# Silu as one ScalarE function, and a head's decay matrix made once and read back, in a gated-delta and retention block

## The chip, the core and the metric

The kernel runs on one core of one Trainium2 chip. Its engines are TensorE (PE in the profile, with PEld for its weight loads), VectorE (DVE), ScalarE (ACT), GpSimd (POOL) and SyncE (SP); each takes its instructions strictly in the order in which they are queued. The metric is the time of one execution in device microseconds (us), as the median of the runs. The kernel before takes 1379.87 us (median of 3 runs, 1377.66 to 1380.05).

## The reference, cut to what matters

One transformer layer on 512 tokens of 1024 features. One projection `xn @ w_in` gives the inputs of two branches. Branch A convolves its q, k and v along the tokens, puts them through silu, and runs a gated delta rule over 8 heads; branch B is a retention over 4 heads. Both are normed and multiplied by a silu gate:

```python
qkv = jax.nn.silu(causal_depthwise_conv(jnp.concatenate([qa, ka, va], axis=-1), conv_a))
...
decay = jnp.exp(jnp.where(causal, g_cum[..., :, None] - g_cum[..., None, :], -jnp.inf))
lower = jnp.where(strict, jnp.einsum('bhncd,bhnmd->bhncm', k_beta, k) * decay, 0.0)
...
attn = jnp.where(causal, jnp.einsum('bhncd,bhnmd->bhncm', q, k) * decay, 0.0)
...
oa = rmsnorm(oa, norm_a) * jax.nn.silu(za.reshape(b, s, A_HEADS, A_DV))
...
ob = rmsnorm(ob, norm_b.reshape(B_HEADS, B_DV)) * jax.nn.silu(gb.reshape(b, s, B_HEADS, B_DV))
```

The decay matrix of a head depends on the gate g alone and is used twice: with the keys (`lower`) and with the queries (`attn`). Two sigmoid gates, the output projection and an MLP with squared ReLU follow.

## The kernel before

All weight products are taken in three matmuls of a high and a low part (`mm3`, L83 to L85). A block of weights, 128 x 1024, is loaded on SP's queue into `raw` (L93, 2 buffers), cast by ACT into `whi` (L113) and subtracted by DVE into `wlo` (L114); whi and wlo have 3 buffers each. So every 24 matmuls PE needs one ACT cast and one DVE subtraction. Products land in 4 PSUM banks `mm`; 3 more banks `dl` and one bank `tr` serve the small products and the transpositions.

A scheduler orders the instructions of every engine by priority (program order, with the weight splits lifted by 200) and by its own model of durations, so each engine's queue interleaves several of the steps below. Where a tile has only one buffer, the writer of the next tile waits for all readers of the last.

Branch A is written in this order: `keys(0)` (heads 0 to 3), `base_inverse(0)`, `values_queries(0)`, `keys(1)` (heads 4 to 7), then for each pair of heads g2 = 0 to 3 `recurrence`, `values_queries(g2 + 1)`, `gated` and `ya_partial`. The steps that the change touches:

- `conv_silu` (L496), called 32 times on 128 x 512 (8 times in keys for kf, 16 for the values, 8 for qf). ACT copies the product into `c_raw` (L501) and scales it into `c_y` (L506), DVE adds three taps (L508), ACT takes the tanh of it into c_raw (L509), DVE makes (tanh + 1) * c_y (L512). The factor one half of silu(x) = x/2 * (tanh(x/2) + 1) sits in the conv weights (L417). PE then transposes the result into the one `tr` bank; for the keys ACT squares it (L523) and copies it into `kd` (L568), which frees that bank.
- `decays(h)` (L525): ACT scales a triangular mask by a column eight times (L531, tiles `tg`, 2 buffers, 4 for `ghi` and 4 for `glo`), PE sums it in two matmuls (L532), ACT takes the exp into `dt` (L534, one buffer). It is called twice for every head, in `keys` and again in `values_queries`: 16 calls.
- The readers of dt: in keys, four DVE products into `mt` (L587, named acc) and four into kd (L590) for each head; in values_queries four products into `at` (L706).
- `gate_rows` (L466), the gate of branch A, 16 tiles: tanh on ACT (L470), (tanh + 1) * z on DVE (L471), then the norm on DVE (L473). `gate` in `outputs` (L914), the gate of branch B, 16 tiles: tanh on ACT (L917), product on DVE (L918). Two tanh more, for the sigmoid gates (L958, L986), stay as they are.
- `double_blocks` uses the buffer of dt for its tile `y` as well.

The exp needs another function table of ACT than Sqrt or Ln; the program loads a table by an instruction of its own (ACT_TABLE_LOAD) wherever the next function is not in the one loaded.

Of the kernel before, what the change touches and what calls it, by code (L numbers as in the profile page):

```python
# [10 lines left out]
F32 = mybir.dt.float32  # L11
# [3 lines left out]
AF = mybir.ActivationFunctionType  # L15
ALU = mybir.AluOpType
# [3 lines left out]
P = 128  # L20
T = 512
# [39 lines left out]
def hybrid_block_kernel(ctx: ExitStack, tc: tile.TileContext, a: dict, out: bass.AP):  # L61
    nc = tc.nc
# [15 lines left out]
    dr = ctx.enter_context(tc.tile_pool(name="dr", bufs=2, space=DRAM))  # L78
# [237 lines left out]
    convw = cp.tile([P, P], F32, name="convw")  # L316
# [39 lines left out]
    with tc.tile_pool(name="xp", bufs=2) as xp:  # L356
# [59 lines left out]
        transpose(pv[:, 1, :], conv_in)  # L416
        nc.vector.tensor_scalar(convw, pv[:, 1, :], 0.5, None, ALU.mult)  # L417
        nc.scalar.copy(later, cmat[:, 2 * P : 3 * P])
# [47 lines left out]
    def gate_rows(pss, o_t, zt):  # L466

        for t in range(4):
            th = zt(t)
            nc.scalar.activation(th, pss[t], AF.Tanh, scale=0.5)  # L470
            nc.vector.scalar_tensor_tensor(th, th, 1.0, pss[t], ALU.add, ALU.mult)  # L471
            for ap, rs, cs in o_t(t):
                nc.vector.scalar_tensor_tensor(ap, ap, rs, th[:, cs], ALU.mult, ALU.mult)  # L473
# [22 lines left out]
    def conv_silu(ps, ch, dst, pool):  # L496
        raw = pool.tile([P, T + 3], F32, tag="c_raw", name="c_raw", bufs=2)
        nc.gpsimd.memset(raw[:, 0:3], 0.0)
        y = pool.tile([P, T], F32, tag="c_y", name="c_y", bufs=2)
        th = raw[:, 0:T]  # L500
        nc.scalar.copy(raw[:, 3 : T + 3], ps)  # L501

        def tap(j):
            return convw[:, j * 32 + ch : j * 32 + ch + 1]

        nc.scalar.activation(y, ps, AF.Copy, scale=tap(3))  # L506
        for j in (2, 1, 0):
            nc.vector.scalar_tensor_tensor(y, raw[:, j : j + T], tap(j), y, ALU.mult, ALU.add)  # L508
        nc.scalar.activation(th, y, AF.Tanh)  # L509
        if dst is None:  # L510
            dst = y
        nc.vector.scalar_tensor_tensor(dst, th, 1.0, y, ALU.add, ALU.mult)  # L512
        return dst
# [11 lines left out]
    def decays(h, pool):  # L525
# [7 lines left out]
        dt = pool.tile([P, 4, P], F32, tag="dt", name="dt")  # L533
        nc.scalar.activation(dt, pd.rearrange("p (c n) -> p c n", c=4), AF.Exp)  # L534
        return dt

# [10 lines left out]
    with tc.tile_pool(name="pa", bufs=1) as pa:  # L547
# [130 lines left out]
        def values_queries(g2, pool):  # L678
# [13 lines left out]
            at = pool.tile([P, 8, P], F32, tag="at", name="at")  # L692
            ssq = pool.tile([P, 8], F32, tag="ssq", name="ssq", bufs=2)
            pss = feature_major(w_in, xs, OFF_QA + h0 * P, 256, 8)
            for hh in range(2):
# [3 lines left out]
                sum_squares(to_tokens(qf[:, hh, :]), ssq[:, 4 * hh : 4 * hh + 4], junk)  # L699
                dt = decays(h, pool)  # L700
                pk = psx.tile([P, 4, P], F32, tag="dl", name="dl", bufs=3)
# [18 lines left out]
        def recurrence(g2, vq, pool):  # L720
# [67 lines left out]
            rstd = pool.tile([P, 8], F32, tag="rstd", name="rstd", bufs=2)  # L788
            nc.vector.scalar_tensor_tensor(rstd, rsqrt(v, 8, "o"), 0.5, rq, ALU.mult, ALU.mult)
            return Rows(  # L790
# [38 lines left out]
    with tc.tile_pool(name="pb", bufs=1) as pb_:  # L829
# [6 lines left out]
        def tmp(name):  # L836
            return pb_.tile([P, T], F32, tag="tm", name=name, bufs=8)
# [68 lines left out]
        def outputs(h, scs):  # L906
# [7 lines left out]
            def gate(t):  # L914
                g = gs[:, t, :]
                th = tmp("g_t")
                nc.scalar.activation(th, g, AF.Tanh, scale=0.5)  # L917
                nc.vector.scalar_tensor_tensor(g, th, 1.0, g, ALU.add, ALU.mult)  # L918

# [18 lines left out]
            rstd = pb_.tile([P, 4], F32, tag="rstd", name="rstd")  # L938
            nc.vector.tensor_scalar(rstd, rsqrt(v, 4, "b"), 0.5, None, ALU.mult)
            for t in range(4):  # L940
# [341 lines left out]
```

## Time and profile before

| | us |
|---|---|
| median of 3 runs | 1379.87 |
| lowest and highest run | 1377.66, 1380.05 |
| the profiled execution, its own time | 1375.68 |
| span from its first to its last instruction | 1374.0 |
| PE busy | 1351.5 |
| DVE busy | 914.0 |
| ACT busy | 652.4 |

The profile is one execution. Busy time is the time in which an engine had an instruction in work; matmuls are pipelined, so their durations overlap, and what one costs in a stream is the distance from its start to the next start. "The chain that ended last" follows the execution back from its last instruction, at each step to what released it. A line in the table of waits reads: this engine's instruction sat idle for that one.

### The profile page before, as it was taken

Reading aid. Unit: us, or ns where it says so; the run is one execution under the profiler, and the core shown is the slowest. Engines: PE = TensorE matmul, PEld = TensorE weight load, DVE = VectorE, ACT = ScalarE, POOL = GpSimd, SP = SyncE. Lnnn points to the kernel's source line nnn. Section 1 sums busy time; section 2 is a strip of 40 time slices with the busy share of each in tenths; the row PEclk is TensorE's granted clock in tenths of the full one; section 3 lists DMA queues with packets and bytes.
Section 4 is the critical chain, followed back from the end, with each engine's and each line's share of the span. In section 5 each row is a group of like instructions: output and inputs, shape, how many; then the busy total and the mean of one; then the engine's idle time right before and its main releaser. Section 6 shows DMA issues by size and latency. Waiting matters only on the chain.

```text
span 1374.0 us, 17717 instructions
## 1 busy us (share of the span) xinstructions
PE 1351.5 (98%) x6598; PEld 1108.3 (81%) x6598; DVE 914.0 (67%) x1599; ACT 652.4 (47%) x1202; POOL 110.6 (8%) x160
## 2 busy tenths in 40 slices
PE   8999999999999999999999999999999999999997
PEld 5888788778887888887888888888889788787886
DVE  5599889963665557567477577575775745828535
ACT  6777564624543323453453343343455646336441
POOL 1112300221012002000000100011101100000000
PEclk9999999999999999999999999999999999999999
DMA  5243625369458447785583872588739843525421
GB/s 161 77 139 120 193 81 172 120 140 241 109 122 173 109 145 163 182 249 180 132 269 112 199 252 93 157 218 176 209 124 233 215 150 104 193 92 166 130 88 62
DMA packets 101656, 214.70 MB, mean 156 GB/s; under 512 B 7135, under 2 KB 20593, under 8 KB 101058
## 3 DMA queue, kind: packets, MB, share of 16 engines
q1 hardware_dynamic: 85616, 170.41, 38.8%
q0 software_dynamic: 15232, 41.90, 16.9%
q8 instruction: 52, 0.85, 0.3%
q10 hardware_dynamic: 722, 1.25, 0.2%
q14 instruction: 34, 0.28, 0.1%
HBM read 207.77 MB, written 64.49 MB: 198 GB/s over the span
## 4 chain that ended last, share of the span: by engine, by line
PE 84%; DVE 9%; ACT 3%; DMA 3%; issue 1%; SPq 0%; DVEq 0%; ACTq 0%
PE mm L85 19%; PE mm L84 19%; PE mm L83 19%; PE mm L238 9%; PE dl L238 8%; PE tr L320 2%; DVE wlo L114 2%; DMA raw<-in_w_in_dram 1%; DVE c_y L508 1%; PE dl L85 1%; PE dl L84 1%; PE dl L83 1%; DVE ffq L1116 1%; ACT whi L113 1%; PE dl L772 1%
## 5 line engine op out<-in xcount | busy, mean ns | idle before, releaser
L114 DVE TENSOR_TENSOR wlo<-raw,whi 128x1024 fp32r<-128x1024 f32 x250 | 305.0, 1222 | 275.6 <-ACT whi L113 274.7
L113 ACT CAST whi<-raw 128x1024 fp32r<-128x1024 f32 x250 | 262.9, 1052 | 439.9 <-PE mm L84 252.5
L84 PE MATMUL mm<-actT,whi 128*128 128x512 f32 (+1 forms) x528 | 207.4, 393 | 1.2 <-DVE actT L354 1.2
L85 PE MATMUL mm<-actT,wlo 128*128 128x512 f32 (+1 forms) x528 | 208.4, 395 | 0.0
L83 PE MATMUL mm<-actT,whi 128*128 128x512 f32 (+1 forms) x528 | 207.0, 393 | 1.0 <-ACT actT L353 1.0
L83 PEld LDWEIGHTS mm<-actT,whi 128*128 128x128 f32 x528 | 100.0, 190 | 20.9 <-ACT actT L353 1.3
L84 PEld LDWEIGHTS mm<-actT,whi 128*128 128x128 f32 x528 | 100.0, 189 | 20.4 <-DVE actT L354 1.4
L85 PEld LDWEIGHTS mm<-actT,wlo 128*128 128x128 f32 x528 | 100.2, 190 | 18.9
L85 PE MATMUL mm<-hn,wlo 128*128 128x512 f32 (+1 forms) x288 | 105.4, 366 | 0.0
L84 PE MATMUL mm<-hn,whi 128*128 128x512 f32 (+1 forms) x288 | 105.3, 366 | 0.0
L83 PE MATMUL mm<-hn,whi 128*128 128x512 f32 (+1 forms) x288 | 105.3, 366 | 0.0
L83 PE MATMUL mm<-og,whi 128*128 128x512 f32 x256 | 99.7, 390 | 0.5 <-DVE zz L471 0.5
L84 PE MATMUL mm<-og,whi 128*128 128x512 f32 x256 | 99.6, 389 | 0.0
L85 PE MATMUL mm<-og,wlo 128*128 128x512 f32 x256 | 99.6, 389 | 0.0
L238 PE MATMUL mm<-whi,xsum 128*128 128x512 f32 x256 | 80.8, 389 | 0.0
L508 DVE SCALAR_TENSOR_TENSOR c_y<-c_raw,convw,c_y 128x512 f32<-128x512 f32 x96 | 70.6, 751 | 3.4 <-ACT c_y L506 2.8
L85 PEld LDWEIGHTS mm<-hn,wlo 128*128 128x128 f32 x288 | 54.3, 189 | 8.8
L83 PEld LDWEIGHTS mm<-hn,whi 128*128 128x128 f32 x288 | 54.3, 189 | 8.7
L83 PE MATMUL mm<-whi,actT 128*128 128x512 f32 x152 | 61.3, 403 | 0.0
L84 PEld LDWEIGHTS mm<-hn,whi 128*128 128x128 f32 x288 | 54.3, 189 | 8.6
L238 PE MATMUL dl<-whi,ffq 128*128 128x512 f32 x192 | 61.1, 389 | 0.0
L238 PE MATMUL dl<-whi,actT 128*128 128x512 f32 x192 | 61.1, 389 | 0.0
(331 smaller groups left out, 2543.8 us busy)
## 6 DMA issues: line engine op xcount, KB each, us to landing
raw<-in_w_in_dram SPq DMA_DIRECT2D x105, 512.0 KB, 4.0
raw<-sums SPq DMA_DIRECT2D x56, 512.0 KB, 4.3
raw<-in_w_up_dram SPq DMA_DIRECT2D x36, 512.0 KB, 4.2
sums<-in_w_in_dram SPq DMA_DIRECT2D x32, 512.0 KB, 5.1
sums<-sums POOLq DMA_DIRECT2D x28, 512.0 KB, 7.5
raw<-in_w_down_dram SPq DMA_DIRECT2D x26, 512.0 KB, 4.4
sums<-in_w_down_dram SPq DMA_DIRECT2D x24, 512.0 KB, 7.4
raw<-in_w_br_a_dram SPq DMA_DIRECT2D x16, 512.0 KB, 4.1
```

The costliest lines, as they stand in the source:

```text
L83: nc.tensor.matmul(ps, lh, rh, start=first, stop=False)
L84: nc.tensor.matmul(ps, lh, rl, start=False, stop=False)
L85: nc.tensor.matmul(ps, ll, rh, start=False, stop=last)
L113: nc.scalar.copy(hi[:, :n], raw[:, :n])
L114: nc.vector.tensor_tensor(lo[:, :n], raw[:, :n], hi[:, :n], ALU.subtract)
L238: m = nc.tensor.matmul(pss[t], lhs[i // 2], rhs[i % 2], start=first and k + i == 0, stop=k + i == 5, skip_group_check=not first,)
L320: nc.tensor.transpose(ps, src, ident)
L508: nc.vector.scalar_tensor_tensor(y, raw[:, j : j + T], tap(j), y, ALU.mult, ALU.add)
L772: nc.tensor.matmul(po[:, hh, :], at[:, 4 * hh + c, :], vn[:, hh, :], start=True, stop=True)
L1116: return nc.scalar.copy(dst[0], r), nc.vector.tensor_tensor(dst[1], r, dst[0], ALU.subtract)
```

## The change

Silu becomes one ACT function: in `conv_silu` it writes the result itself, in `gate_rows` it reads PSUM and writes zz, in `gate` it works in place. The DVE product behind it is gone in all three, and so are the halves (L417, L789, L939). `decays` also stores dt to device memory, on ACT's queue, and `values_queries` reads it back, on ACT's queue, into the buffers of `tg`, instead of making it again.

```diff
         transpose(pv[:, 1, :], conv_in)
-        nc.vector.tensor_scalar(convw, pv[:, 1, :], 0.5, None, ALU.mult)
+        nc.vector.tensor_copy(convw, pv[:, 1, :])
...
         for t in range(4):
             th = zt(t)
-            nc.scalar.activation(th, pss[t], AF.Tanh, scale=0.5)
-            nc.vector.scalar_tensor_tensor(th, th, 1.0, pss[t], ALU.add, ALU.mult)
+            nc.scalar.activation(th, pss[t], AF.Silu)
...
         y = pool.tile([P, T], F32, tag="c_y", name="c_y", bufs=2)
-        th = raw[:, 0:T]
...
-        nc.scalar.activation(th, y, AF.Tanh)
         if dst is None:
             dst = y
-        nc.vector.scalar_tensor_tensor(dst, th, 1.0, y, ALU.add, ALU.mult)
+        nc.scalar.activation(dst, y, AF.Silu)
         return dst
...
         dt = pool.tile([P, 4, P], F32, tag="dt", name="dt")
         nc.scalar.activation(dt, pd.rearrange("p (c n) -> p c n", c=4), AF.Exp)
+        kept_decays[h] = dr.tile([P, 4, P], F32, tag=f"dt{h}", name="dts", bufs=1)
+        nc.scalar.dma_start(kept_decays[h], dt)
+        return dt
+
+    kept_decays = {}
+
+    def decays_again(h, pool):
+        dt = pool.tile([P, 4, P], F32, tag="tg", name="dt", bufs=2)
+        nc.scalar.dma_start(dt, kept_decays[h])
         return dt
...
             ssq = pool.tile([P, 8], F32, tag="ssq", name="ssq", bufs=2)
+            dts = [decays_again(h0 + hh, pool) for hh in range(2)]
             pss = feature_major(w_in, xs, OFF_QA + h0 * P, 256, 8)
...
-                dt = decays(h, pool)
+                dt = dts[hh]
...
-            nc.vector.scalar_tensor_tensor(rstd, rsqrt(v, 8, "o"), 0.5, rq, ALU.mult, ALU.mult)
+            nc.vector.tensor_tensor(rstd, rsqrt(v, 8, "o"), rq, ALU.mult)
...
             def gate(t):
                 g = gs[:, t, :]
-                th = tmp("g_t")
-                nc.scalar.activation(th, g, AF.Tanh, scale=0.5)
-                nc.vector.scalar_tensor_tensor(g, th, 1.0, g, ALU.add, ALU.mult)
+                nc.scalar.activation(g, g, AF.Silu)
...
-            nc.vector.tensor_scalar(rstd, rsqrt(v, 4, "b"), 0.5, None, ALU.mult)
+            nc.vector.tensor_copy(rstd, rsqrt(v, 4, "b"))
```

The scheduler then orders the queues anew. In the changed kernel's numbering the Silu of conv_silu is L509, the exp L531, the store L533, the reading back L540, the masks L528, the two copies of the product L499 and L504.

On ACT at the start of keys(0), from the cast of a weight block to the second key's Silu, there stands before:

```order
L113 CAST whi<-raw 128x1024
L509 ACTIVATE c_raw<-c_y 128x512 x2
L534 ACTIVATE dt<-dl 128x512
L501 COPY c_raw<-mm 128x512
L523 ACTIVATE junk,ssk<-tr 128x128
```

and now, from the squares of the first key on (kf is the keys' result, junk the squares for its norm, kd the copy that frees the bank tr; the first load and the Silus of the first two keys stand directly behind the same cast, six rows ahead of this piece):

```order
L499 COPY c_raw<-mm 128x512
L520 ACTIVATE junk,ssk<-tr 128x128
L504 ACTIVATE c_y<-mm,convw 128x512
L520 ACTIVATE junk,ssk<-tr 128x128
L574 COPY kd<-tr 128x512
L531 ACT_TABLE_LOAD
L531 ACTIVATE dt<-dl 128x512
L520 ACTIVATE junk,ssk<-tr 128x128
L509 ACT_TABLE_LOAD
L509 ACTIVATE kf<-c_y 128x512
L520 ACTIVATE junk,ssk<-tr 128x128
L509 ACTIVATE kf<-c_y 128x512
```

The exp has moved from the place right behind the first two keys' tanh to behind the first copy into kd, with a load ahead of it and one behind it, ahead of the Silus of the third and the fourth key.

On ACT at the end of keys(0), where the exps of heads 1 to 3 stand among the first products of the values, before:

```order
L534 ACTIVATE dt<-dl 128x512
L531 ACTIVATE tg<-cmat,ghi 128x128 x4
L531 ACTIVATE tg<-cmat,glo 128x128 x4
L501 COPY c_raw<-mm 128x512
L534 ACTIVATE dt<-dl 128x512
L506 ACTIVATE c_y<-mm,convw 128x512
L501 COPY c_raw<-mm 128x512
L506 ACTIVATE c_y<-mm,convw 128x512
L531 ACTIVATE tg<-cmat,ghi 128x128 x4
L534 ACTIVATE dt<-dl 128x512
```

and now:

```order
L531 ACT_TABLE_LOAD
L531 ACTIVATE dt<-dl 128x512
L528 ACTIVATE tg<-cmat,ghi 128x128
L533 DMA dts<-dt 128x512
L528 ACTIVATE tg<-cmat,ghi 128x128 x3
L528 ACTIVATE tg<-cmat,glo 128x128 x3
L531 ACTIVATE dt<-dl 128x512
L528 ACTIVATE tg<-cmat,glo 128x128
L533 DMA dts<-dt 128x512
L113 CAST whi<-raw 128x1024
L499 COPY c_raw<-mm 128x512
L504 ACTIVATE c_y<-mm,convw 128x512
```

The three exps stand behind one load, each is followed by its store, and the exp of the next head writes the buffer that the store reads.

On ACT in the second half of keys(1), where the exps of heads 5 to 7 stand beside the first values of values_queries(1), there is now (before, there were no loads and no DMAs):

```order
L531 ACTIVATE dt<-dl 128x512
L113 CAST whi<-raw 128x1024
L533 DMA dts<-dt 128x512
L509 ACT_TABLE_LOAD
L509 ACTIVATE c_y<-c_y 128x512
L531 ACT_TABLE_LOAD
L531 ACTIVATE dt<-dl 128x512
L113 CAST whi<-raw 128x1024
L533 DMA dts<-dt 128x512
L509 ACT_TABLE_LOAD
L509 ACTIVATE c_y<-c_y 128x512
```

Here three loads stand within eleven rows, since an exp lies between two Silus.

## Rows read from the trace of the kernel before

**Rows 1.** The profile's page: busy time by engine, and the chain by engine.
```profile
PE 1351.5 (98%) x6598; PEld 1108.3 (81%) x6598; DVE 914.0 (67%) x1599; ACT 652.4 (47%) x1202; POOL 110.6 (8%) x160
...
PE 84%; DVE 9%; ACT 3%; DMA 3%; issue 1%; SPq 0%; DVEq 0%; ACTq 0%
```

**Rows 2.** Busy time by stage; a stage's line gives its length, then busy us.
```profile
core 0: us, PE busy (x) PEld busy (x) DVE busy (x) ACT busy (x) POOL busy (x), PEclk, DMA share, GB/s
44.00:90.00 46.00, 46.00 (x228) 37.47 (x227) 36.69 (x82) 36.75 (x101) 3.79 (x11) 1.00 0.35 98
...
122.00:172.00 50.00, 48.24 (x319) 38.65 (x319) 45.78 (x124) 30.69 (x86) 10.65 (x22) 1.00 0.48 152
...
395.00:470.00 75.00, 73.92 (x333) 60.09 (x332) 41.65 (x74) 27.34 (x53) 9.72 (x10) 1.00 0.75 153
```

**Rows 3.** What PE waited for: us in total, times, longest.
```profile
PE dl L238 <- DVE wlo L114: 4.2, 3, 1.4
...
PE tr L320 <- DVE c_y L512: 1.1, 1, 1.1
...
PE tr L320 <- DVE kf L512: 0.7, 1, 0.7
PE mm L83 <- DVE zz L471: 0.5, 1, 0.5
```

**Rows 4.** PE in order of time around two calls of decays: start, duration.
```profile
90.70 0.40 PE L85 MATMUL mm<-actT,wlo 128*128 128x512 f32 x1
90.94 0.62 PE L532 MATMUL dl<-tg,later 128*128 128x512 f32 x2
91.39 0.39 PE L83 MATMUL mm<-actT,whi 128*128 128x512 f32 x1
...
385.79 0.71 PE L532 MATMUL dl<-tg,later 128*128 128x512 f32 x2
386.44 0.94 PE L704 MATMUL dl<-qf,kf 128*128 128x128 f32 x6
```

**Rows 5.** Groups by line: count, busy us, mean ns of one, idle before.
```profile
L532 PE MATMUL dl<-tg,later 128*128 128x512 f32 x32 | 11.8, 430 | 0.0
...
L531 ACT ACTIVATE tg<-cmat,ghi 128x128 fp32r<-128x128 f32 x64 | 22.3, 402 | 1.9 <-DVE ghi L456 1.2 <-PE dl L532 0.7
...
L470 ACT ACTIVATE zz<-mm 128x512 f32<-128x512 f32 x16 | 9.5, 596 | 7.3 <-PE mm L85 7.3
...
L534 ACT ACTIVATE dt<-dl 128x512 f32<-128x512 f32 x16 | 9.5, 592 | 1.9 <-DVE kd L590 1.0 <-PE dl L532 0.9
...
L590 DVE TENSOR_SCALAR kd<-kd,rk,dt 128x128 f32<-128x128 f32 x32 | 10.9, 341 | 0.0
...
L471 DVE SCALAR_TENSOR_TENSOR zz<-zz,mm 128x512 f32<-128x512 f32 x16 | 10.8, 678 | 0.0
L512 DVE SCALAR_TENSOR_TENSOR c_y<-c_raw,c_y 128x512 f32<-128x512 f32 x16 | 10.8, 682 | 2.4 <-ACT c_raw L509 2.4
...
L918 DVE SCALAR_TENSOR_TENSOR gs<-g_t,gs 128x512 f32<-128x512 f32 x16 | 10.6, 685 | 0.0
```

**Rows 6.** ACT in order of time around a table load.
```profile
28.13 1.28 ACT L429 ACT_TABLE_LOAD   x1
29.43 0.23 ACT L429 ACTIVATE beta<-ba 128x32 f32<-128x32 f32 x1
```

**Rows 7.** DMA issues: count, KB each, median us from issue to landing; one ACT issue's duration.
```profile
raw<-in_w_in_dram SPq DMA_DIRECT2D x105, 512.0 KB, 4.0
...
raw<-in_w_br_a_dram SPq DMA_DIRECT2D x16, 512.0 KB, 4.1
...
dec<-in_c_decay_dram POOLq DMA_DIRECT2D x4, 256.0 KB, 3.0
...
out_dram<-acc ACTq DMA_DIRECT2D x4, 256.0 KB, 2.1
...
1349.96 0.35 ACTq L1252 DMA_DIRECT2D out_dram<-acc  x1
```

**Rows 8.** Pieces of the chain in order of time, two loads: start, us.
```profile
396.38 10.07 DMA raw<-in_w_br_a_dram
...
418.76 9.12 DMA raw<-in_w_in_dram
```

## The prediction

> **What bounds the kernel now.** First the busy times and the chain of the page [rows 1]: PE is busy 98% of the span and holds 84% of the chain that ended last, DVE 67% and ACT 47% busy. A saving on ACT or DVE alone is therefore worth only the idle time of PE that it ends, and a saving on PE is worth its full length as long as nothing else starts to hold PE up. Next I read the busy time by stage [rows 2], since the change lies almost wholly in branch A, the first 470 us. There PE is busy without a gap in the first keys (44 to 90 us) and 48.24 of 50 us in the second keys (122 to 172). ACT is busy 36.75 of 46 us in the first of these stages and 30.69 of 50 in the second; DVE is at 45.78 of 50 in the second, so DVE has little room there and ACT little in the first. Last I read the waits of PE [rows 3]. PE is idle for 22.5 us of the span in all (1374.0 - 1351.5), and three of its waits name the DVE lines that the change deletes: 1.1 us on the values (L512), 0.7 us on the keys (L512) and 0.5 us on the gate (L471). The largest entry, 4.2 us on wlo in the MLP, is not touched.
>
> **PE: the decay products.** Eight of the 16 calls of decays go, with two matmuls each: 16 matmuls. Matmuls overlap, so I take the distance between starts [rows 4] and not the group's mean duration of 430 ns [rows 5]: from 90.94 to 91.39 us two of them take 0.45 us, 0.23 each, as long as the matmul ahead of them (90.70 to 90.94); from 385.79 to 386.44 two take 0.65 us, 0.33 each, between small fp32 products. Both surroundings occur about equally, so I take 0.27: 16 x 0.27 = 4.3 us, all on the bound engine, between 16 x 0.23 = 3.7 and 16 x 0.33 = 5.3.
>
> **DVE: the products behind the tanh.** 32 in conv_silu at 682 ns, 16 at L471 at 678 and 16 at L918 at 685 [rows 5]: 21.8 + 10.8 + 11.0 = 43.6 us of DVE. PE hides nearly all of it already. What is on the path is the three waits of [rows 3], 1.1 + 0.7 + 0.5 = 2.3 us. Two of them could come back as waits for the Silu, the third cannot: the gate's PSUM bank is now read by one ACT instruction only. Bounds 0.5 and 2.3; I take 2.3, and book what comes in their place below. The other edits (a copy where a scaling by one half stood, at convw and the two rstd) are one DVE instruction for one: nothing.
>
> **ACT: what goes.** A call of decays costs ACT eight masks of 402 ns and an exp of 592 ns [rows 5], about 3.8 us by durations; eight calls are some 30 us. All of it lies in the values_queries stages, where ACT has room, so on the path it is nothing. A Silu takes the place of a tanh in each of 64 instructions. The trace has no Silu; its nearest rows are the tanh at 596 ns and the exp at 592 ns on the same 128 x 512 [rows 5], two functions with one duration, so I take no difference, and leave a longer Silu to a rival.
>
> **ACT: the table loads.** The order of the changed kernel has 16 loads where the old has five: two Silu-to-exp turns and back in keys(0), three in keys(1), and the first Silu, 11 loads more. One takes 1.28 us, and the function behind it starts 1.30 us after the load [rows 6]: 11 x 1.30 = 14.3 us of ACT. Five of them fall into the stage from 44 to 90 us: 36.75 + 5 x 1.30 = 43.3 of 46 us, and six DMA issues of at most 0.35 us [rows 7] make 45.4. ACT is nearly full there. What covers it: PE has 24 matmuls of 0.23 us for every weight block, and the new order shows that the scheduler has moved PE's work accordingly. Between the transpositions of the second and the third key PE now has 27 weight matmuls, 6.1 us by the distance in [rows 4], where it had 9 (2.0 us) and a decay product. Two loads and the exp that moved in between, 2 x 1.30 + 0.59 = 3.2 us, fit into the 4.1 us added. Without that cover they would be 3.2 us of idle PE. The cover is thin at one place in each keys stage: the product of the third head needs the PSUM bank that the exp of the second head frees, and that exp now stands behind a load. Bounds 0 to 1.30 each, 2.6 for both; I take 0.5 each.
>
> The Trainium skill prices this higher: its page "ScalarE: Activation LUTs", section "What ACT_TABLE_LOAD costs", gives a switch of tables as about 1283 ns and a drain of about 1380 ns behind it, 2.66 us in total, and its rule is to do all calls of one table before the next. The load's 1.28 us agrees with [rows 6]; a drain behind it does not, since there the next function starts 0.02 us after the load's end. By the page the 11 loads would be an estimated 29.3 us of ACT, and the keys stage would overflow; by the row they just fit.
>
> **ACT's queue and the device memory.** Each exp is followed by a store of 256 KB, and dt has one buffer: the next head's exp, already in ACT's queue, now waits for the store's landing too. Before, it waited for DVE's eight readers, 8 x 0.34 = 2.7 us [rows 5]. A store lands 2.1 us after its issue from ACT, or 3.0 like a load of that size on POOL's queue [rows 7], plus 0.35 us of issue: 2.5 to 3.4, so 0 to 0.7 us more than the readers, at four exps (heads 2, 3, 6 and 7): 0 to 2.8 us. Behind the waiting exp stand a weight cast, which PE needs once in 24 matmuls, and the copies that free PSUM. I take half of it, 1.4 us. The readings back are issued a whole stage ahead of their readers (the first pair behind the exps of keys(0), the others at the end of the stage before), against 2.1 to 3.0 us of flight: nothing. One stands ahead of the second query's Silu and waits for DVE's readers of an older matrix; PE has some 16 matmuls (3.7 us) of cover there: nothing.
>
> **The sum.** -4.3 - 2.3 + 1.0 + 1.4 = -4.2 us. Against the profiled execution that is a span of 1374.0 - 4.2 = 1369.8 us and a time of 1375.68 - 4.2 = 1371.5; that execution ran 4.2 us below the median of the runs, and on the median the same difference gives 1379.9 - 4.2 = 1375.7 us. Best corner: -5.3 - 2.3 = -7.6, 1372.3. Worst corner of the terms: -3.7 - 0.5 + 2.6 + 2.8 = +1.2, 1381.1.
>
> **Rivals.** (1) *ACT becomes the bound in the keys stages* (slower). For it: 45.4 of 46 us busy in the first of them, ACT works in order, and every load stands between a PSUM copy and a Silu that PE waits for; a load can only begin when the instruction ahead has ended. Against it: the matmuls moved in between, and ACT's room in the second stage (30.69 + 6 x 1.30 = 38.5 of 50). It decides for slower once eight of the 11 loads show on PE (8 x 1.30 = 10.4, less 4.3 + 2.3 = 6.6, is +3.8); with nine, 11.7 - 6.6 = +5.1: 1385.0 us. By the price of a switch on the page of the Trainium skill named above, an estimated four loads would do. (2) *Given back at the weight loads* (no change). Two loads around 396 and 419 us take 10.07 and 9.12 us on the chain [rows 8] where such loads take 4.0 to 4.1 in the median [rows 7], because the sums of weight blocks fill the DMA engines; PE loses 1.1 of its 75 us there [rows 2]. A PE that arrives earlier may wait there for what it won. Against it: a load is issued when PE and DVE have freed its buffer, so it moves along. Price: all but the 0.5 of the gate, 1379.4 us. (3) *All waits go and none comes*: -4.3 - 2.3 = -6.6, 1373.3 us; the scheduler had PE without a gap from 44 to 90 us before. (4) *It doesn't do what it says*: if Silu took ACT twice as long as the tanh, 64 x 0.6 = 38 us would return to ACT, more than decays gives back; in the keys stage 8 x 0.6 = 4.8 us on a full engine would show, -4.2 + 4.8 = +0.6: 1380.5 us. Nothing in the trace speaks for it but that it has no Silu.
>
> **How the numbers follow.** Forecast 0.50 (1375.7); (1) 0.13 (1385.0); (2) 0.20 (1379.4); (3) 0.12 (1373.3); (4) 0.05 (1380.5). About 0.2%, 2.8 us, is what a measurement of this kernel can tell from no change. The forecast is faster in 9 of 10 of its cases, (3) always, (2) rarely: 0.58 faster. Slower comes from (1) and a few of (4): 0.13. The rest, 0.29, is the same. The range reaches from the best corner, 1372.0, over (2) and (4) to the worst corner of the terms, 1381.5, and leaves (1) out with part of the tails.
>
> **What would show it.** In the profile after: PE with 16 matmuls fewer on the decay line and 64 instructions fewer on DVE; 16 loads of 1.28 us; a Silu near 0.6 us. Right, if PE's waits in the first 470 us are no longer than before, with the waits on L471 and L512 gone. Term by term wrong, if PE waits for the Silu of a key or value (loads), if the exp's idle time names the store (buffer), or if the waits around 400 us on weight loads have grown by what was won (2). The whole is wrong, if the stage from 44 to 90 us, counted to the same matmul, has become more than 2 us longer.

## The result: slower, with PE waiting for the exps

The changed kernel takes 1382.7 us in the median of its eleven runs (1380.1 to 1390.5), the kernel before 1378.7 in eleven runs beside them: a ratio of 1.0038, 95% interval 1.0026 to 1.0050. One of the eleven runs, 1501.1 us at a granted clock of 0.85 where the others have 0.99 to 1.00, is left out of that range and of the ratio. The forecast was 1375.7, 4.2 us less than before, and its range ended at 1381.5; the measured difference is +4.0 us, so the sign was wrong and the range too short. The profiled execution of the changed kernel took 1382.7 us with a span of 1381.0.

What the change takes away is gone. First the page's busy times by engine, as in [rows 1]:

```profile
PE 1352.9 (98%) x6582; PEld 1107.1 (80%) x6582; DVE 878.6 (64%) x1535; ACT 644.4 (47%) x1141; POOL 107.3 (8%) x160
```

Then the groups of the lines that the change touches, with the columns of [rows 5]:

```profile
L509 ACT ACTIVATE c_y<-c_y 128x512 f32<-128x512 f32 x16 | 10.1, 631 | 11.4 <-DVE c_y L506 11.3
L590 PE MATMUL dl<-kf 128*128 128x128 f32 x64 | 9.9, 299 | 4.6 <-ACT dt L531 4.6
L470 ACT ACTIVATE zz<-mm 128x512 f32<-128x512 f32 x16 | 9.3, 596 | 5.5 <-PE mm L85 5.5
L509 ACT ACT_TABLE_LOAD x6 | 7.7, 1283 | 0.1
L531 ACT ACT_TABLE_LOAD x5 | 6.4, 1283 | 0.1
L529 PE MATMUL dl<-tg,later 128*128 128x512 f32 x16 | 6.0, 416 | 0.2 <-ACT tg L528 0.2
L531 ACT ACTIVATE dt<-dl 128x512 f32<-128x512 f32 x8 | 4.8, 598 | 5.8 <-DMA dts<-dt 5.8
```

PE has 16 matmuls fewer than in [rows 1] and DVE 64 instructions fewer; a Silu takes 596 ns from PSUM and 631 from SBUF; the 11 new loads take 1283 ns each. The last row is the news: ACT stood idle in front of an exp for 5.8 us until a store of the matrix made ahead of it had landed. What PE waited for between 40 and 470 us (us in total, times, longest):

```profile
PE dl L590 <- ACT dt L531: 4.6, 3, 2.1
PE dl L759 <- ACT vn L754: 1.6, 2, 1.3
PE mm L85 <- DVE wlo L114: 0.6, 1, 0.6
PE mm L83 <- ACT c_y L504: 0.4, 1, 0.4
```

The three waits of [rows 3] on L512 and L471 are gone. In their place the product of a head's keys (L590) waits three times for the exp, 4.6 us. Both sides of these waits follow, ACT first, then PE (start, duration, idle before and its releaser):

```profile
77.60 0.41 ACTq L533 DMA_DIRECT2D dts<-dt  x1
...
81.79 0.60 ACT L531 ACTIVATE dt<-dl 128x512 f32<-128x512 f32 x1 [1.86 <-DMA dts<-dt]
...
150.34 1.05 ACT L113 CAST whi<-raw 128x1024 fp32r<-128x1024 f32 x1 [2.04 <-DMA raw<-in_w_in_dram]
151.40 1.28 ACT L531 ACT_TABLE_LOAD   x1
152.70 0.60 ACT L531 ACTIVATE dt<-dl 128x512 f32<-128x512 f32 x1
...
153.33 0.34 ACTq L533 DMA_DIRECT2D dts<-dt  x1
...
159.77 0.60 ACT L531 ACTIVATE dt<-dl 128x512 f32<-128x512 f32 x1 [3.91 <-DMA dts<-dt]
```

```profile
82.44 0.49 PE L590 MATMUL dl<-kf 128*128 128x128 f32 x2 [1.12 <-ACT dt L531]
...
150.81 0.39 PE L84 MATMUL mm<-actT,whi 128*128 128x512 f32 x1
153.35 2.00 PE L590 MATMUL dl<-kf 128*128 128x128 f32 x8 [2.15 <-ACT dt L531]
155.00 0.77 PE L85 MATMUL mm<-actT,wlo 128*128 128x512 f32 x1
155.58 0.63 PE L83 MATMUL mm<-actT,whi 128*128 128x512 f32 x1
156.00 0.63 PE L84 MATMUL mm<-actT,whi 128*128 128x512 f32 x1
156.43 0.60 PE L85 MATMUL mm<-actT,wlo 128*128 128x512 f32 x1
156.86 0.41 PE L83 MATMUL mm<-actT,whi 128*128 128x512 f32 x1
157.10 0.40 PE L84 MATMUL mm<-actT,whi 128*128 128x512 f32 x1
...
160.42 1.16 PE L590 MATMUL dl<-kf 128*128 128x128 f32 x8 [1.30 <-ACT dt L531]
```

Two of the three exps (81.79 and 159.77) waited for a store, issued 4.2 and 6.4 us earlier; PE waited 1.12 and 1.30 us for them, 2.4 in all. The one at 152.70 did not wait for a store: it stood in ACT's queue behind a cast that waited 2.04 us for a weight block, and behind a table load, and PE waited 2.15 us for it. After PE's 2.15 us without work, a weight matmul follows the one before it after 0.42 us (155.58 to 156.00) where 0.24 us is usual (156.86 to 157.10). The windows show why:

```profile
122.00:172.00 50.00, 45.49 (x283) 36.51 (x283) 42.35 (x119) 38.12 (x93) 8.98 (x18) 0.97 0.52 155
...
153.40:156.80 3.40, 3.40 (x12) 3.07 (x13) 3.40 (x10) 2.34 (x8) 0.10 (x1) 0.51 0.99 266
```

The granted clock in the second row is 0.51: half, 1.2 instead of 2.4 GHz, for 3.4 us, which gives 1.7 us of PE away. The first row is the second keys stage of [rows 2]: PE busy 45.49 us instead of 48.24, with a clock of 0.97.

### The profile page after: what moved, and what is told of

The parts are those of the page before. It is cut to its first block, busy times and chain, and to the rows that moved or that the text cites. A ratio compares the mean times of both kernels' runs of the same rounds, so it can differ in the third digit from the quotient of the medians.

```text
span 1381.0 us, 17590 instructions
## 1 busy us (share of the span) xinstructions
PE 1352.9 (98%) x6582; PEld 1107.1 (80%) x6582; DVE 878.6 (64%) x1535; ACT 644.4 (47%) x1141; POOL 107.3 (8%) x160
## 5 line engine op out<-in xcount | busy, mean ns | idle before, releaser
L83 PE MATMUL mm<-actT,whi 128*128 128x512 f32 (+1 forms) x528 | 207.8, 395 | 0.9 <-ACT actT L353 0.6
L85 PE MATMUL mm<-actT,wlo 128*128 128x512 f32 (+1 forms) x528 | 208.0, 396 | 0.6 <-DVE wlo L114 0.6
L83 PEld LDWEIGHTS mm<-actT,whi 128*128 128x128 f32 x528 | 100.6, 191 | 21.5 <-ACT c_y L504 1.9
L85 PEld LDWEIGHTS mm<-actT,wlo 128*128 128x128 f32 x528 | 100.7, 191 | 19.9 <-DVE wlo L114 1.0
L85 PE MATMUL mm<-hn,wlo 128*128 128x512 f32 (+1 forms) x288 | 105.4, 366 | 0.0
L83 PE MATMUL mm<-hn,whi 128*128 128x512 f32 (+1 forms) x288 | 105.3, 366 | 0.0
L83 PE MATMUL mm<-og,whi 128*128 128x512 f32 x256 | 99.6, 389 | 0.0
L85 PE MATMUL mm<-og,wlo 128*128 128x512 f32 x256 | 99.6, 389 | 0.0
L85 PEld LDWEIGHTS mm<-hn,wlo 128*128 128x128 f32 x288 | 54.3, 189 | 8.8
L83 PE MATMUL mm<-whi,actT 128*128 128x512 f32 x152 | 61.1, 402 | 0.3 <-DVE tb L1003 0.3
L83 PEld LDWEIGHTS mm<-hn,whi 128*128 128x128 f32 x288 | 54.3, 189 | 8.6
```

What stands on the lines that cost most here:

```text
L83: nc.tensor.matmul(ps, lh, rh, start=first, stop=False)
L85: nc.tensor.matmul(ps, ll, rh, start=False, stop=last)
```

## A balance of PE over branch A

Weight matmuls (L83 to L85) come in the same number in every version, so I count from the 97th (about 38 us) to the 1441st (about 480 us), which contains what the change touches. Length, time in which PE is idle, and time at half clock, from the traces; "rest" is the length less the idle time less half of the time at half clock. Times are us. A row is one traced execution, whose own time lies up to 3.3 us off the median beside it (e6: 1379.4 against 1376.2).

| kernel | median | length | PE idle | half clock | rest |
|---|---|---|---|---|---|
| before | 1378.7 | 439.8 | 3.4 | 0 | 436.4 |
| before, second trace (e12) | | 441.8 | 5.2 | 0 | 436.6 |
| changed | 1382.7 | 444.4 | 8.3 | 3.4 | 434.3 |
| changed, second trace (e11) | | 446.2 | 10.6 | 3.4 | 433.9 |
| tanh in conv (e2) | 1375.2 | 437.1 | 5.6 | 0 | 431.6 |
| kept only (e4) | 1376.7 | 439.2 | 7.2 | 0 | 432.1 |
| no store (e6) | 1376.2 | 438.8 | 5.9 | 0 | 432.8 |
| no loads (e5) | 1384.7 | 446.0 | 9.6 | 6.8 | 433.0 |
| two buffers (e1) | 1390.7 | 456.1 | 11.6 | 23.9 | 432.5 |
| second exp (e9) | 1392.9 | 454.3 | 13.9 | 13.7 | 433.5 |
| Silu only (e8) | 1390.0 | 450.8 | 7.4 | 13.7 | 436.6 |
| before, two buffers (e14) | 1384.6 | 446.1 | 9.3 | 0 | 436.8 |
| tanh in conv, two buffers (e3) | 1386.2 | 447.8 | 8.1 | 13.7 | 432.8 |
| tanh in keys (e7) | 1381.4 | 444.2 | 8.3 | 6.8 | 432.5 |
| tanh in conv, second exp (e10) | 1383.5 | 444.3 | 6.6 | 13.7 | 430.8 |
| changed, 512-byte rows (e13) | 1385.4 | 448.6 | 11.5 | 6.8 | 433.7 |
| tanh in conv, 512-byte rows (e15) | 1377.0 | 439.7 | 6.5 | 3.4 | 431.5 |
| Silu behind the last exp (e16) | 1379.9 | 442.7 | 8.7 | 3.4 | 432.3 |

The mean length of the two traces of the changed kernel is 445.3, of the kernel before 440.8: +4.5 us, close to the +4.0 of the medians. PE's own work has fallen by 2.1 to 2.7 us; 5.1 us of idle time (9.4 against 4.3) and 1.7 of half clock are added. In every kernel with the eight calls gone the rest is smaller, in e2 and e4 by 4.3 to 5.0, as forecast. That the changed kernel shows only half of it does not lie in the decay products: from start to next start, with idle time and half clock taken off, they take 8.75 us in the kernel before, 4.07 in the changed one and 4.05 in e2, so 4.7 us less in both. Its other matmuls stand further apart than before, the weight matmuls by 0.5 to 1.0 us in sum and the products of vt and rt by 0.6. I read times in the following by these columns: they say of which kind a loss is, where a median says only how large.

## Experiments

S, L, C, T and O are the theories that the expectations name: the store's landing, the table loads, the clock, the traffic, the order.

**e1, two buffers for the decay matrix** (in `decays`):

```
-        dt = pool.tile([P, 4, P], F32, tag="dt", name="dt")
+        dt = pool.tile([P, 4, P], F32, tag="st", name="dt", bufs=2)
```

> The changed kernel with one edit: the decay matrix of a head is made in the two buffers of tag st, which lie idle in the keys stages, in place of the single buffer of tag dt, so that an exp no longer waits for the store of the head before it. Theory S (the exp waits for a store that lands late): the two waits of PE on the product L590 behind such an exp, 1.29 us near 81 us and 1.47 near 159, go: the changed kernel's 1382.7 us less 2.8, 1379.9. Theory L (the table loads ahead of the exps and Silus hold PE up): the loads stay, so at most 0.5 us of change, 1382.2 to 1382.7, and the largest wait, 2.3 us near 151, stays. Theory C (PE's idle time near 151 lets its clock fall to half for 3.4 us): as L for this run.

1390.7 us, ratio 1.0079 (1.0066 to 1.0092): 8 us slower than the changed kernel, although no exp waits for a store. PE's waits between 40 and 172 us, then a window of the same trace:

```profile
PE dl L590 <- DVE acc L593: 2.2, 2, 2.0
PE mm L83 <- ACT c_y L504: 1.5, 2, 1.1
PE mm L85 <- DVE wlo L114: 1.4, 1, 1.4
```

```profile
157.80:166.30 8.50, 8.50 (x35) 6.18 (x34) 4.67 (x7) 3.29 (x5) 2.84 (x5) 0.50 0.90 271
```

Two products now come close behind another and wait for DVE to empty their PSUM banks, and PE waits 1.4 us for a weight split of DVE. The clock is at half for the whole 8.5 us of this window, and for 23.9 us in branch A. S as I had put it has fallen: the wait went, but the scheduler had put the work around it elsewhere, so this run doesn't show what the wait cost.

**e2, tanh in the convolutions; e3, the same with two buffers; e4, the second part of the change alone.** In e2 and e3 `conv_silu` is the one of the kernel before:

```
-        nc.scalar.activation(dst, y, AF.Silu)
...
+        nc.scalar.activation(th, y, AF.Tanh)
...
+        nc.vector.scalar_tensor_tensor(dst, th, 1.0, y, ALU.add, ALU.mult)
```

The half in the conv weights is back with it. e4 has the two gates as before also.

> The changed kernel with tanh and the product on DVE back in the 32 convolutions of keys, values and queries; Silu stays in the gates, the decay matrix is still stored and read back. No Silu stands between the exps any more, so 10 of the 11 added table loads go. Theory L: the loss of 8.3 us (4.0 slower, and 4.3 of PE's work saved) lies mostly in the loads, so the time falls to 1376 or less. Theory S: the store still delays two exps by 2.8 us; only the 1.3 us of load in the wait near 151 and the clock's 1.7 go, 1379.7; the waits on the product behind the tanh come back with 1.8 us, 1381.5. Theory T (the traffic of storing and reading 4 MB holds up the weight loads): no change, 1382.7.

> Both edits at once: tanh and DVE product in the convolutions, and two buffers for the decay matrix. Theories S and L add up: 1382.7 less 2.8 less 3.0 to 6.7, 1373.2 to 1376.9, faster than the kernel before by 2 to 5 us. By L alone it is within 0.5 us of the run with tanh in the convolutions and one buffer; by S alone within 0.5 us of the run with two buffers and Silu everywhere. Theory T: 1382.7.

> The kernel before with only the second part of the change: the decay matrix of a head is stored once and read back, and tanh with its product on DVE stays everywhere, so there are five table loads as before. The prediction's terms: 16 matmuls fewer, -4.3 us, store waits +1.4: 1378.7 - 2.9 = 1375.8 us. Theory S: -4.3 + 2.8, 1377.2. Theory L: no loads, so -4.3 alone, 1374.4. Theory T (traffic): 1380 or more.

e2: 1375.2 us, 0.9980 (0.9969 to 0.9991), faster than both kernels and the best of this study. e3: 1386.2 us, 1.0050 (1.0038 to 1.0062). e4: 1376.7 us, 0.9991 (0.9980 to 1.0001). The two edits of e3 do not add up: two buffers cost 11 us here, with PE waiting 4.6 us for weight splits of DVE and 13.7 us at half clock. T is out, since e2 and e4 store and read back the same 4 MB. e2 agrees with L in size, and this is the point at which one could have stopped with a story that e5 does not bear out. e4 holds the second part of the change to the prediction's own terms: they gave 1375.8 and it took 1376.7. PE's waits between 40 and 172 us in e2:

```profile
PE dl L531 <- DVE acc L595: 1.3, 1, 1.3
PE dl L592 <- ACT dt L533: 1.1, 1, 1.1
PE tr L320 <- DVE kf L511: 1.0, 1, 1.0
```

The second is again the product behind an exp that waits for a store; in e4 it waits 1.1 us too. So the same eight stores cost PE 1.1 us in these two orders, and 2.4 in the first trace of the changed kernel's.

**e5, no loads; e6, no store; e7, tanh in the keys alone; e8, the first part of the change alone.** e5 takes `AF.Tanh` for `AF.Exp` in `decays`, which makes another matrix. e6, in which seven heads read a wrong matrix, and e7, whose conv weights of the keys have the half back:

```
-        nc.scalar.dma_start(kept_decays[h], dt)
+        if h == 0:
+            nc.scalar.dma_start(kept_decays[h], dt)
...
-        nc.scalar.dma_start(dt, kept_decays[h])
+        nc.scalar.dma_start(dt, kept_decays[0])
```

```
...
+        if 8 <= ch < 16:
...
+            nc.scalar.activation(th, y, AF.Tanh)
+            nc.vector.scalar_tensor_tensor(dst, th, 1.0, y, ALU.add, ALU.mult)
+        else:
+            nc.scalar.activation(dst, y, AF.Silu)
```

e8 calls `decays` twice per head, without store and read-back.

> The changed kernel with tanh in place of exp in the making of the decay matrix (what is computed there is another function, so the decay is left out in effect), since tanh stands in the same table as Silu: the 10 loads between Silu and exp go, everything else, Silu everywhere, the store and the read-back, stays. Theory L (the loads hold PE up): the loss goes as it did with tanh in the convolutions, and the DVE products stay away, 1374 to 1376 us. Theory S (the store's late landing): 1380 to 1382. Theory O (it is the order of the work around the exps, not the time of the loads): 1380 or more although no load is left.

> The changed kernel with the store of the decay matrix left out for heads 1 to 7; every read-back reads what head 0 stored (seven heads get a wrong decay). 16 loads stay, and an exp waits only for DVE's readers. Theory S: the two waits of 1.3 and 1.5 us on the product behind an exp that waited for a store go, 1379.9 us. Theory L: the wait near 151 us and the half clock stay, and so most of the loss: 1380 to 1382.7. Theory O: up to 8 us in either direction, as the two buffers showed, by where the order puts the products L590.

> The changed kernel with tanh and the DVE product in the eight convolutions of the keys alone, where the exps stand; values, queries and gates keep Silu, and the decay matrix is stored and read back. Three table loads are added in place of 11. Theory L: as fast as with tanh in all convolutions or a little faster, since the wait on the values' product (1.1 us) does not come back: 1374 to 1375.2 us, below the kernel before by 3.3 to 4.5. Theory S: the store's two waits stay, 1377. Theory O: between 1374 and 1385 by the order.

> The first part of the change alone: Silu everywhere, and the decay matrix made twice as before, nothing stored or read back. 25 table loads are added in place of 11, the 14 others in the values and queries stages where ACT is busy 55 to 62 of 100 us. If every load costs PE what the 11 cost on average, 0.75 us: 1378.5 - 2.3 + 18.8 = 1395 us. If only those in the two keys stages cost: 1378.5 - 2.3 + 8.3 = 1384.5. If the loss came from the store and the read-back and not from the loads: 1376.2.

e5: 1384.7 us, 1.0041 (1.0024 to 1.0059), no faster than the changed kernel although ten loads are gone. So a loss of this size does not need the loads, and L as the whole cause has fallen; what they cost in the changed kernel's own order e5 does not say, since the order of its work is another too. ACT in its second keys stage, then PE's waits between 40 and 172 us:

```profile
144.03 0.33 ACTq L533 DMA_DIRECT2D dts<-dt  x1
...
150.02 0.60 ACT L531 ACTIVATE dt<-dl 128x512 f32<-128x512 f32 x1 [3.76 <-DMA dts<-dt]
```

```profile
PE dl L590 <- ACT dt L531: 2.9, 1, 2.9
PE dl L666 <- issue: 1.7, 1, 1.7
```

The store landed 6 us after its issue, and the one wait for it is longer than each of the three it replaced. e6: 1376.2 us, 0.9987 (0.9978 to 0.9997), with all 16 loads: without stores the loss goes. Its order is another too, so the 6.5 us are not the store's price. In that trace PE waits 1.0 us for a Silu that stands behind a weight cast, and 1.1 us for an exp that stands behind a load and, ahead of it, a cast that waited 1.19 us for a weight block. e7: 1381.4 us, 1.0024 (1.0010 to 1.0037), missed by all but O: with three added loads, PE waits 4.5 us for a transfer of the blocks of the inverse (rn) at 157 us, and the clock is at half for 6.8 us behind it. e8: 1390.0 us, 1.0087 (1.0069 to 1.0106), between the two prices of L. Its idle time is 7.4 us, about that of e4; what it has is 13.7 us at half clock. It stores nothing, so a loss does not need the stores either. In the stage from 44 to 90 us PE is busy for 45.93 us with loads among its exps: there they are hidden, as forecast.

**e9, a second exp for the store; e10, the same with tanh in the convolutions.**

```
...
+        out = pool.tile([P, 4, P], F32, tag="st", name="out", bufs=2)
+        nc.scalar.activation(out, pd.rearrange("p (c n) -> p c n", c=4), AF.Exp)
-        nc.scalar.dma_start(kept_decays[h], dt)
+        nc.scalar.dma_start(kept_decays[h], out)
```

> The changed kernel with a second exp per head, into the two buffers of tag st, from which the store goes out; the matrix that DVE reads stays in its own single buffer and no exp of it waits for a store any more. Costs ACT eight exps of 0.6 us, 16 loads stay. Theory S, as the run without the store left it (1376.2): the store's late landing costs some 6.5 us, waits and half clock together, so 1376 to 1378 us with everything computed. Theory O (the order of the work decides, not the wait): anything from 1376 to 1390, with PE idle for over 2 us at another place in the second keys stage and the clock at half behind it.

> Tanh and the DVE product in the convolutions (no table load between the exps) and the second exp for the store. Theories S and L together: below the run with tanh in the convolutions alone (1375.15), where the store still costs a wait of 1.1 us on the product L592: 1373 to 1374.5 us. Theory O: 1375 to 1386, as with two buffers.

e9: 1392.9 us, 1.0105 (1.0091 to 1.0120). e10: 1383.5 us, 1.0036 (1.0025 to 1.0048). Both miss by S: no exp waits for a store, and PE waits elsewhere, in e9 4.2 us for weight casts on ACT and 3.3 for the emptying of PSUM by ACT, in e10 2.0 us on L670 with 13.7 us at half clock.

**e11 and e12, the changed kernel and the one before, unchanged, for second traces.**

> The changed kernel once more, unchanged, for a second trace of the same program. If its loss is fixed by its order of work, the waits on the product L590 near 81, 151 and 159 us stand there again within 0.5 us, and the time is 1380 to 1384. If the half clock near 153 us comes and goes by the execution, it is missing here or longer, and the time differs from 1382.7 by as much (3.4 us at half clock are 1.7 us).

> The kernel before once more, unchanged, for a second trace. If the 1.7 us that the changed kernel loses at the loads of w_out near 1000 us are the chance of one execution, they appear here or are missing in the changed kernel's second trace; if they belong to the change, this trace has PE without a gap there, as the first. No half clock between 25 and 1370 us.

They took 1382.0 and 1383.4 us. PE's waits between 40 and 470 us in e11, then in e12 between 980 and 1010:

```profile
PE dl L590 <- ACT dt L531: 5.9, 3, 2.4
PE dl L759 <- ACT vn L754: 2.1, 2, 1.8
PE tr L320 <- ACT qf L509: 0.8, 1, 0.8
```

```profile
PE mm L83 <- ACT keep L113: 2.3, 1, 2.3
```

The three waits on L590 belong to the program: they stand there again, at 79, 149 and 156 us, the last of them 2.44 us long where it was 1.30. The half clock belongs to the execution: in e11 it is missing at 153 us and stands at 434 us, behind a wait of 1.8 us for vn. What the first trace of the changed kernel lost at the loads of w_out near 1000 us is chance: in e12 the kernel before loses more there (PE busy 26.97 of 30 us against 29.97 in its first trace). Behind these 2.3 us the clock of the kernel before falls to half for 3.4 us as well, which the expectation had ruled out: falling is nothing that only the changed kernel does.

**e13 and e15, the same order and a slower store; e14, two buffers in the kernel before and with them another order, without any work added.** The stored matrix is laid out by quarters, so that a transfer moves 512 bytes a row, not 2 KB. On every engine the instructions stand in the same order as without this edit.

```
-  kept_decays[h] = dr.tile([P, 4, P], F32, tag=f"dt{h}", name="dts", bufs=1)
+  kept_decays[h] = dr.tile([4, P, P], F32, tag=f"dt{h}", name="dts", bufs=1).rearrange("c p n -> p c n")
```

e14 is the kernel before with the first diff of this section.

> The changed kernel with the stored decay matrix laid out so that the store and the read-back move rows of 512 bytes in place of 2 KB; every engine's instructions stand in the same order, so only the transfers differ. The store landed 4.3 us after its issue in the median and 6.4 at the most. Theory S: four times as many packets make it land some 2 us later, and each of the exps near 82, 159 and 164 us moves back by as much: 3 to 6 us more, 1385.5 to 1388.5. Theory O: the landing plays no part, 1382 to 1383.5. Theory L: as O.

> The kernel with tanh in the convolutions (1375.15 us) and the same layout of 512-byte rows; the order of every engine is the same as there. Theory S: its one wait of PE for an exp behind a store (1.1 us) grows by about 2 us, and the clock may fall behind it: 1377 to 1379. Theory O: 1375 to 1376.

> The kernel before with the decay matrix in the two buffers of tag st; nothing stored, no table load added, only one wait of the exp on DVE's readers taken away and with it another order of the work. Theory O: the time moves by several us although nothing is added, to 1382 or more, as with two buffers in the changed kernel, by PE's idle time in the second keys stage and half clock behind it. Theories S and L: nothing of theirs is in this kernel, 1377 to 1379.

e13: 1385.4 us, 1.0045 (1.0032 to 1.0057); e15: 1377.0 us, 0.9988 (0.9975 to 1.0000). By medians that is 2.7 and 1.8 us more than without the edit, but the intervals overlap those of the changed kernel and of e2, so the times alone don't prove it. The trace of e13 does show the mechanism, in PE's waits, ACT's waits and ACT in order of time:

```profile
PE dl L590 <- ACT dt L531: 7.7, 3, 3.7
```

```profile
ACT dt L531 <- DMA dts<-dt: 8.1, 2, 4.6
```

```profile
151.59 1.05 ACT L113 CAST whi<-raw 128x1024 fp32r<-128x1024 f32 x1 [1.20 <-DMA raw<-in_w_in_dram]
...
154.58 0.40 ACTq L533 DMA_DIRECT2D dts<-dt  x1
...
161.78 0.60 ACT L531 ACTIVATE dt<-dl 128x512 f32<-128x512 f32 x1 [4.59 <-DMA dts<-dt]
```

PE's three waits in e13:

```profile
83.58 0.49 PE L590 MATMUL dl<-kf 128*128 128x128 f32 x2 [2.71 <-ACT dt L531]
...
154.60 1.16 PE L590 MATMUL dl<-kf 128*128 128x128 f32 x8 [1.31 <-ACT dt L531]
...
162.43 1.28 PE L590 MATMUL dl<-kf 128*128 128x128 f32 x8 [3.66 <-ACT dt L531]
```

The two exps wait 8.1 us for the stores, not 5.3 to 5.8. For them, the first and the third row, PE waits 6.4 us (2.71 + 3.66), where it was 2.4 in the changed kernel's first trace and 3.4 (0.99 + 2.44) in e11. The two stores land 5.7 and 7.1 us after their issue, 2.4 and 3.0 us later in sum than in those traces (S had some 2 us each). With the order held, what a store takes longer arrives at PE, here whole and more. In e15 PE's one such wait is 2.2 us, not 1.1, and the clock falls to half for 3.4 us behind it, where e2 kept it.

The wait in the second row goes by something else. In the first trace of the changed kernel, in e11 and in e13 the cast ahead of that exp waited 2.04, 2.34 and 1.20 us for its weight block, and PE waited 2.15, 2.43 and 1.31. The store that e13 slows is not in it, and the table load, which stands in it each time, has not changed. A late weight block sets this wait; no run takes the load away with the order held, so what the load adds is not shown.

e14: 1384.6 us, 1.0039 (1.0025 to 1.0053). Nothing is stored, loaded or computed otherwise; an exp may run one matrix further ahead of DVE's readers, the tiles y and st share their buffers differently, and the kernel loses 6.3 us, more than by the whole change. The only wait of PE in its trace that names one of these buffers is 0.2 us on st; the larger ones below name other tiles. PE's waits between 40 and 470 us:

```profile
PE tr L320 <- DVE c_y L512: 2.4, 1, 2.4
PE dl L752 <- ACT vn L747: 2.1, 1, 2.1
PE dl L654 <- DMA rn<-scr: 1.5, 2, 1.3
```

**e16, Silu behind the last exp.** The condition of e7 becomes `ch < 2 or 8 <= ch < 20`, so that the values and queries of heads 0 and 1 have tanh too.

> The kernel with tanh in the convolutions (1375.15 us), but with Silu in the 18 convolutions of values and queries of heads 2 to 7, which lie behind the last exp; eight table loads in place of six, PE's order the same up to the second keys stage's end. If Silu in itself is neutral for PE: 1374.5 to 1375.5 us. If the DVE products that it saves (18 of 0.68 us) were holding PE up in the stages from 172 us on: down to 1373. If another order costs there too: 1376 to 1380.

1379.9 us, 1.0013 (1.0002 to 1.0025). From the 97th to the 481st weight matmul it stays within 0.03 us of e2. Behind that PE waits 2.7 us for DVE on the decay product, 1.3 in e2; then one Silu of a later value is put ahead of the last exp, with a load on each side, and PE waits 2.2 us for the next Silu, which stands behind that exp and a third load. The order is another here too, and Silu did not stay behind the last exp, so this run does not price Silu by itself.

## The forecast, point by point

- **PE's 16 matmuls, -4.3: right on their own line**, where 4.7 us are gone. The rest column falls by 4.3 to 5.0 us in e2 and e4, in the changed kernel by 2.1 to 2.7: some half of the saving went into wider distances between other matmuls, for which the sum had no term.
- **The three waits, -2.3: right.** None is left.
- **Silu like tanh: right**, 596 ns from PSUM and 631 from SBUF, as the tanh on the same lines. Rival (4) is out.
- **The table loads, +1.0: the place right, the size not.** 11 loads of 1283 ns. The thin place that the prediction names, the third head's product behind the second head's exp, costs PE nothing in the first keys stage, and 2.15 and 2.43 us in the second (first trace and e11), above its bound of 1.30. The excess goes with the late weight block ahead of the load, which no term had. Rival (1) is out: ACT is busy 37.29 of 46 us in the stage from 44 to 90 us, and 39.5 at the most with its six DMA issues, not 45.4, since work moved out of the stage with the order. I had taken the stage's other work as fixed.
- **The store and the single buffer, +1.4: the step that failed.** Two exps waited for a store, not four, and PE waited 2.4 and 3.4 us for them (first trace and e11), where four waits of at most 0.7 us were allowed. The bounds took a landing of 2.1 to 3.0 us from [rows 7], of transfers at the end of the program and of loads. In the keys stages the two stores landed 4.1 and 6.4 us after their issue, beside weight loads (DMA share 0.95 from 77.60 to 81.80 and 0.99 from 153.40 to 156.80), while one that was issued at 160.40 landed after 2.0. And I had PE wait through the weight cast behind the exp, so only half was to show; in fact the product L590 waits for the exp itself, because the exp frees the PSUM bank. The part "ACT: the table loads" names that bank, the part on the store does not. The step fails in this order, not in every one: e2 and e4 have the same stores and lose 1.1 us to them.
- **The two terms together** booked 2.4 us of waiting for the exp (1.0 + 1.4); L590 waited 4.6 and 5.9.
- **What the sum had no term for.** First, the clock: both traces of the changed kernel have 3.4 us at half clock, 1.7 us, behind a wait. Secondly, shorter waits of PE on wlo, c_y, qf, vt and tg, 1.7 and 2.2 us. The waits on vn, behind a cast that waits for a weight block, explain nothing of the difference: 1.6 and 2.1 us against 0.7 and 2.8 before. That is the place of rival (2), in a spread that the kernel before has too; what it describes, time lost at a late weight block, came instead in the second keys stage.
- **The balance.** The idle time grew by 5.1 us where the sum had it grow by 0.1 (-2.3 + 1.0 + 1.4): 5.3 at L590 and 2.0 in the shorter waits, less the 2.1 that went (means of two traces each). With 1.7 of half clock and some 2 of PE's saving that did not show, these make up the 8 us between -4.2 and +4.0.
- **The signs.** The exp's idle time names the store, as the prediction asked for "buffer". Its sign for the whole being wrong did not show: counted to the same matmul, the stage from 44 to 90 us is 46.4 and 46.1 us long against 45.8. The two larger waits lie in the second keys stage.
- **The range** had the store's and the loads' mechanisms at its worst corner, +1.2; its ends, 1372.0 and 1381.5, lie 0.3 and 0.4 us outside the corners worked out from the terms, 1372.3 and 1381.1. It had no case in which another order of the same work is worth 6 us, as in e14. Which share of the 4 us is the store's and which the order's is open: holding the order shows that the landing counts (e13), not what would be left without it.

The Trainium skill's page "ScalarE: Activation LUTs", section "What ACT_TABLE_LOAD costs", adds a drain of about 1380 ns to the load. In these traces no such time stands on either side of a load: the load at 151.40 starts 0.01 us after the end of the cast ahead of it (150.34 + 1.05), and the exp behind it at 152.70, 0.02 us after its end. The Trainium skill's rule to group calls by table, in the section "Table sets: the hidden batching unit" of the same page, points at e2, the best kernel here; but e5, grouped as well, is slow, and e6, with all 16 loads, is not, so grouping alone does not decide.

## What to carry to other kernels

Where a store leaves from a buffer that its producer needs again, price its landing from transfers under the load of that same stage, and ask who waits for the producer's PSUM bank, not only what is queued behind it. Where a scheduler orders the engines, an edit has two prices, its own and that of the new order. A control that adds no work and changes the order (e14) shows how large the second can be, one that keeps the order (e13) shows whether a mechanism counts at all; without them a bisection can point at the wrong part, and even with them the shares may stay open, as here. On an engine that is busy 98% of the time, count a wait of some 2 us at more than its length, since PE may come out of it at half clock.

## What the runs showed of the hardware

The granted clock fell to half (0.50 and 0.51 in the windows shown) behind idle stretches of PE between 1.4 us (e1, at 84 us) and 4.5 us (e7), for 3.4 us in the changed kernel and for at least 8.5 us on end in e1; that last fall, at 156 us, stands shortly after the clock had come back, behind 0.5 us of idle time. It did not fall behind others as long: 2.43 and 2.44 us in e11, 2.62 in e4. The same program lost it at 153 us in one execution and at 434 in the next. At half clock weight matmuls follow each other after 0.42 us, not 0.24. A store of 256 KB took 2.0 to 6.4 us from issue to landing in the first trace of the changed kernel, and 2.3 to 7.1 in rows of 512 bytes (e13).
